# The last feed-forward product taken by k tiles first, and the first operands of the second half made inside the last quad

## The chip, the cores and the metric

The kernel runs on one core of one Trainium2 chip. The metric is the device time of one launch, in microseconds. Five engines run side by side, each through its own list of instructions in order: PE (matrix products; its weight loads are PEld), DVE and ACT (elementwise work), POOL (a slower elementwise engine) and SP, which here only issues DMAs.

## The reference, cut to what matters

One transformer block on x (1024 tokens of 1024 channels, fp32), a token mixer and then a gated feed-forward. The change touches only the feed-forward and the final norm:

```python
a, g = jnp.split(h @ w_ffn_in, 2, axis=-1)      # h: 1024 x 1024, w_ffn_in: 1024 x 5632
y    = (jax.nn.silu(g) * a) @ w_ffn_out          # w_ffn_out: 2816 x 1024
x    = x + g2 * y
out  = _rmsnorm(x, final_norm_g)                 # over the 1024 channels of a token
```

## The kernel before, in words

Products are fp32 made of three passes: each operand is split into a high part (a cast, on ACT, L637) and a low part (raw minus high, on DVE, L638), and PE multiplies high by high, high by low and low by high (`PASS`). Each pass of a 128x128 by 128x512 step is one matmul. Big products are done by a 2x2 block scheme with seven block products instead of eight, which needs sums and differences of blocks before and after.

The first half of the feed-forward runs 22 "quads" (`todo`, `run_quads`). A quad makes 128 rows of a and 128 rows of g for all 1024 tokens from seven products of 12 matmuls: A11 (`ahead_1`), S3, A12 (`ahead_2`, called by `others` as `mid`), S2, S1, A22 and S4. Its weights come as two raw tiles (`weights`, L689), are split (`weights_a`, L236/L237) and summed and split again (`weights_s`, L700 to L710). After S2, S1, A22 and S4 DVE adds the products up (L741, L744, L747, L750), POOL one of them (L742), ACT applies silu (L1257), DVE multiplies (L1261), and the result goes to DRAM as `actd`. Each of the four results of a quad is 128x512.

The second half is act @ w_ffn_out by 512x512 quarters with k split in 11 pairs of tiles. Seven block products run in the order P1, P7, P2, P6, P5, P4, P3 (`quarter`, L1285), each 11 k tiles x 4 token tiles x 3 passes = 132 matmuls into four PSUM banks, k outermost. `prepared(name)` loads the operands of k + 1 (L1213; an activation tile and a weight tile of 256 KB each), combines them where the scheme asks for it (L1227, L1231, L1235, L1240), and splits those of k. Raw tiles alternate between a pool of three buffers (named wr) and one of four (wr2), the same two pools that the quads' weights use; split tiles live in a pool of 40 (named s). While a product runs, the steps in its `side` list are interleaved: results of earlier products are taken out of PSUM and joined to the residual (L1300, L1301).

Two places matter here. `f_hook` runs after a quad. In quad 20 (counted from 0, the last but one) it makes the row of g2 (`row_of`: 16 small matmuls into two PSUM banks, L1006, and two copies, L1007) and the operands of P1 for k = 0, with the loads for k = 1. And the last product, P3, has a loop of its own: all 11 operands are prepared first, with the sums of P4's result (L1354) and `finish` of token tiles 4 to 7 between them; then token tile by token tile all k are multiplied (L1368), and each of the token tiles 0 to 3 is joined and finished: two sums of squares on ACT (L1307), a square root on POOL (L172), two scalings on DVE (L1311) and two stores (L1312).

The order of instructions on each engine is set by a scheduler that starts from the order of the program text: what stands earlier in the text takes buffers first.

Of the kernel before, what the change touches and what calls it, by code (L numbers as in the profile page):

```python
# [29 lines left out]
NF = DFF // P  # L30
# [3 lines left out]
def block_kernel(  # L34
# [63 lines left out]
    def gbank(shape=(P, 512)):  # L98
        return psg.tile(list(shape), F32, tag="g", name=nm("g"))
# [527 lines left out]
    def pe(ins):  # L627

        if last_pe[0] is not None:
            tc.add_manual_dep(ins.ins, last_pe[0].name, mybir.DependencyInfo(mybir.DependencyClass.NoSync, mybir.DependencyReason.DATA), reason="pe")  # L630
        last_pe[0] = ins.ins
        return ins

    def parts_of(raw, shape=(P, 2, 512)):

        hi, lo = slot(list(shape), F32R), slot(list(shape), F32R)
        nc.scalar.copy(hi, raw)  # L637
        nc.vector.tensor_sub(lo, raw, f(hi))  # L638
        return hi, lo
# [45 lines left out]
    def weights(w, cols):  # L685
        got = []
        for c0 in cols:
            t = raw_w([P, KT, P])
            nc.sync.dma_start(t, w[:, c0:c0 + P].rearrange("(k p) f -> p k f", p=P))  # L689
            got.append(t)  # L690
        return got

    def weights_a(va):
        hi, lo = split_w(va, [P, KT, P])
        return {"A11": (hi[:, 0:4, :], lo[:, 0:4, :]), "A12": (hi[:, 4:8, :], lo[:, 4:8, :])}

    def weights_s(va, ga, ops, eng):
        a11, a12, a21, a22 = va[:, 0:4, :], va[:, 4:8, :], ga[:, 0:4, :], ga[:, 4:8, :]
        s32, s14 = slot([P, 2, 4, P]), slot([P, 2, 4, P])
        nc.vector.tensor_sub(s32[:, 0], a11, a21)  # L700
        nc.vector.tensor_sub(s32[:, 1], a22, s32[:, 0])
        eng.tensor_add(s14[:, 0], s32[:, 1], a11)
        eng.tensor_sub(s14[:, 1], a12, s32[:, 1])
        for t, names in ((s32, ("S3", "S2")), (s14, ("S1", "S4"))):
            hi, lo = parts_of(t, (P, 2, 4, P))
            for i, name in enumerate(names):
                ops[name] = hi[:, i], lo[:, i]
        both = slot([P, 2, 4, P], F32R)
        nc.scalar.copy(both[:, 0], a22)
        nc.vector.tensor_sub(both[:, 1], a22, f(both[:, 0]))  # L710
        ops["A22"] = both[:, 0], both[:, 1]

    def product(ps, wts, mov, start):
        for k in range(4):
            for i, (a, b) in enumerate(PASS):
                pe(nc.tensor.matmul(ps, wts[a][:, k, :], mov[k // 2][b][:, k % 2, :], start=start and k == 0 and i == 0, stop=k == 3 and i == 2, skip_group_check=True))  # L716

    def tmp(s):
        return small.tile([P, 512], F32, tag="ev", name=nm(s), bufs=ev_bufs)

    def ahead_1(q, op, get_bank):
        q["A"] = get_bank()
        product(q["A"], q["ops"]["A11"], op["B11"], True)
        if q.get("p1") is None:
            q["p1"] = tmp("p1")
        nc.scalar.copy(q["p1"], q["A"])

    def ahead_2(q, op):
        product(q["A"], q["ops"]["A12"], op["B21"], False)

    def others(q, op, sink, mid=None):

        ops, p1 = q["ops"], q["p1"]
        X, Y, q7, u3 = banks[1](), banks[1](), tmp("q7"), tmp("u3")
        product(X, ops["S3"], op["T3"], True)
        nc.scalar.copy(q7, X)  # L736
        if mid:
            mid()
        sink(1, 1, q["A"])
        product(X, ops["S2"], op["T2"], False)  # L740
        nc.vector.tensor_add(u3, X, p1)  # L741
        nc.gpsimd.tensor_sub(q7, u3, q7)  # L742
        product(Y, ops["S1"], op["T1"], True)
        nc.vector.tensor_add(u3, Y, u3)  # L744
        sink(2, 2, u3)
        product(X, ops["A22"], op["T4"], False)
        nc.vector.tensor_add(p1, X, p1)  # L747
        sink(2, 1, p1)
        product(Y, ops["S4"], op["B22"], False)
        nc.vector.tensor_add(q7, Y, q7)  # L750
        sink(1, 2, q7)
# [12 lines left out]
    def run_quads(op, todo, quads, hook=None):  # L764

        for fi, (w, cols, sink) in enumerate(todo):
            if fi < len(quads):
                if fi:
                    weights_s(*weights(w, cols), quads[fi]["ops"], nc.vector)
                others(quads[fi], op, sink)  # L770
            else:
                va, ga = weights(w, cols)
                q = {"ops": weights_a(va)}
                weights_s(va, ga, q["ops"], nc.gpsimd)
                ahead_1(q, op, banks[0])
                others(q, op, sink, lambda: ahead_2(q, op))
            if hook:
                hook(fi)

    def half(t):  # L780
        return slice((t - 1) * 512, t * 512)
# [217 lines left out]
    def row_of(col):  # L999

        row = slot([P, D])
        for hf in range(2):
            pb = gbank((P, 4, P))
            for j in range(4):
                k = 4 * hf + j
                nc.tensor.matmul(pb[:, j, :], col[:, k:k + 1].to_broadcast([P, P]), ident, start=j == 0, stop=True, skip_group_check=True)  # L1006
            nc.vector.tensor_copy(row[:, hf * 512:(hf + 1) * 512], pb.rearrange("p j i -> p (j i)"))  # L1007
        return row

    next_small("small_h")  # L1010
    run_quads(h_op, todo, quads)


    KH = NF // 2
# [201 lines left out]
    def operands(name, k):  # L1216

        k2 = k + KH
        s = sk[k // 2][:, k % 2, :]
        if name == "P1":  # L1220
            return raw_tile(act_q(k, 0), w_q(k, 0))
        if name == "P2":
            return raw_tile(act_q(k2, 0), w_q(k2, 0))
        if name == "P7":
            t, r = raw_tile(act_q(k, 0), wsum[k]["T3"]), tmp("a21")
            nc.sync.dma_start(r, act_q(k, 1))
            nc.vector.tensor_sub(t[:, 0, :], t[:, 0, :], r)  # L1227
            nc.scalar.copy(s, t[:, 0, :])
        elif name == "P6":
            t = raw_tile(act_q(k2, 1), wsum[k]["T2"])  # L1230
            nc.vector.tensor_sub(t[:, 0, :], t[:, 0, :], s)  # L1231
            nc.scalar.copy(s, t[:, 0, :])
        elif name == "P5":
            t = raw_tile(act_q(k, 0), wsum[k]["T1"])
            nc.vector.tensor_add(t[:, 0, :], t[:, 0, :], s)  # L1235
        elif name == "P4":
            t = raw_tile(act_q(k2, 1), wsum[k]["T4"])
        else:
            t = raw_tile(act_q(k2, 0), w_q(k2, 1))
            nc.vector.tensor_sub(t[:, 0, :], t[:, 0, :], s)  # L1240
        return t

    def prepared(name):

        t = operands(name, 0)
        for k in range(KH):
            t, now = operands(name, k + 1) if k + 1 < KH else None, t
            yield parts_of(now)
# [15 lines left out]

    def f_hook(fi):
        nonlocal g2r
        if fi == NF - 2:
            g2r = row_of(g2)
            early.append(next(gen))

# [8 lines left out]
    def quarter(gen, banks, start, side=(), per=2):  # L1279

        side = list(side)
        for k, o in enumerate(gen):
            for tt in range(4):
                for i, (a, b) in enumerate(PASS):
                    pe(nc.tensor.matmul(banks[tt], o[b][:, 0, tt * P:(tt + 1) * P], o[a][:, 1, :], start=start and k == 0 and i == 0, stop=k == KH - 1 and i == 2, skip_group_check=True))  # L1285
            if k >= 1:
                for _ in range(per):
                    if side:
                        side.pop(0)()
        for s in side:  # L1290
            s()
# [6 lines left out]
    def join(xt, sl, src):  # L1298
        t = tmp("gj")
        nc.vector.tensor_mul(t, src, g2r[:, sl])  # L1300
        nc.vector.tensor_add(xt[:, sl], xt[:, sl], t)  # L1301
# [14 lines left out]
    def later(fn, *tiles):  # L1316
        return [lambda tt=tt: fn(tt) for tt in range(4)]

    A, X = [gbank() for _ in range(4)], [bank() for _ in range(4)]
# [28 lines left out]
        nc.vector.tensor_add(u3[tt], Y[tt], u3[tt])  # L1348
        join(fin[4 + tt], rh, u3[tt])

    quarter(prepared("P4"), X, False, later(c22), 1)

    def c21(tt):
        nc.vector.tensor_add(p1[tt], X[tt], p1[tt])  # L1354
# [1 line left out]
        finish(4 + tt)  # L1356


    side = later(c21)
    o = []  # L1360
    for k, parts in enumerate(prepared("P3")):
        o.append(parts)
        if k >= 2 and side:
            side.pop(0)()
    for tt in range(4):
        for k in range(KH):
            for i, (a, b) in enumerate(PASS):
                pe(nc.tensor.matmul(Y[tt], o[k][b][:, 0, tt * P:(tt + 1) * P], o[k][a][:, 1, :], start=False, stop=k == KH - 1 and i == 2, skip_group_check=True))  # L1368
        join(fin[tt], rh, Y[tt])
        finish(tt)  # L1370

# [31 lines left out]
```

## Time and profile before

| what | us |
|---|---|
| device time, median of 3 runs (lowest, highest) | 1780.68 (1780.16, 1782.38) |
| device time of the profiled execution | 1779.25 |
| its span, first to last instruction | 1777.5 |
| PE busy in the span | 1712.9 (96%) |
| DVE, ACT, POOL busy | 1137.3, 668.5, 214.4 |

The profiled execution has 1.75 us around its span and lies 1.43 us below the median. In the profile a line such as L638 is a line of the kernel, a tile's name stands without its number, and "out<-in" says what is written from what. PE's matmuls overlap: the start of one to the start of the next is the time that one takes, and the length printed is longer by the end of its pipeline. A bracket at the end of a row says how long the engine was idle before it, and whose end released it.

### The profile page before, as it was taken

To read this page: it belongs to the slowest core of one execution; us is meant where nothing else is said; L and a number is where in the kernel's file an instruction comes from. 1 tells how busy PE (TensorE), PEld (TensorE's weight loads), DVE (VectorE), ACT (ScalarE), POOL (GpSimd) and SP (SyncE) were. 2 spreads that over 40 slices of the span, in tenths; PEclk is the share of its full clock that TensorE was granted. 3 is DMA by queue.
4 is the path that set the end of the run, shared out by engine and by line. 5 is a ranking of instruction groups with operands and counts; after the bars stand their busy time and mean duration, and the time that the engine had idled before them with its cause. 6 is when DMAs were issued, how large, how long until landed. Compare 5 with 4: busy or idle time off the path is not lost. (4 is left out here: it accounts for less than half of the span.)

```text
span 1777.5 us, 21603 instructions
## 1 busy us (share of the span) xinstructions
PE 1712.9 (96%) x8162; PEld 1407.4 (79%) x8162; DVE 1137.3 (64%) x1559; ACT 668.5 (38%) x974; POOL 214.4 (12%) x193
## 2 busy tenths in 40 slices
PE   8899999999899999999999999899999999899996
PEld 3887888887678888887888888678888888688885
DVE  7686595866964554377756745985555553646795
ACT  6663423423443433234322213533333332445352
POOL 2220000000112352000000000022212211100001
PEclk9999999999999999999999999999999999999998
DMA  9511234052354453487868942243222222568472
GB/s 342 153 36 36 95 108 178 24 178 60 113 165 125 137 171 119 143 307 243 269 209 298 325 159 83 69 124 92 83 75 92 83 76 79 178 226 287 144 249 95
DMA packets 219961, 267.89 MB, mean 151 GB/s; under 512 B 11920, under 2 KB 142032, under 8 KB 219856
## 3 DMA queue, kind: packets, MB, share of 16 engines
q1 hardware_dynamic: 219040, 265.08, 45.0%
q8 instruction: 64, 1.05, 0.2%
q0 software_dynamic: 720, 1.40, 0.2%
q14 instruction: 41, 0.34, 0.1%
q10 hardware_dynamic: 96, 0.02, 0.0%
HBM read 205.64 MB, written 60.82 MB: 150 GB/s over the span
## 5 line engine op out<-in xcount | busy, mean ns | idle before, releaser
L716 PE MATMUL m<-s,s 128*128 128x512 f32 x1320 | 310.8, 392 | 13.7 <-DVE s L638 4.1
L716 PEld LDWEIGHTS m<-s,s 128*128 128x128 f32 x1320 | 247.9, 189 | 70.8 <-DVE s L638 5.8
L273 PE MATMUL m<-s,whi 128*128 128x512 f32 (+1 forms) x832 | 253.2, 385 | 1.4 <-ACT s L992 0.7
L237 DVE TENSOR_TENSOR wlo<-wr,whi 128x1024 fp32r<-128x1024 f32 x92 | 112.4, 1224 | 195.1 <-ACT whi L236 188.4
L716 PE MATMUL g<-s,s 128*128 128x512 f32 x960 | 225.8, 393 | 8.0 <-ACT q L736 4.1
L716 PEld LDWEIGHTS g<-s,s 128*128 128x128 f32 x960 | 180.0, 189 | 50.5 <-ACT q L736 6.9
L273 PEld LDWEIGHTS m<-s,whi 128*128 128x128 f32 x832 | 154.9, 190 | 32.4 <-ACT s L992 1.6
L236 ACT CAST whi<-wr 128x1024 fp32r<-128x1024 f32 x92 | 96.4, 1051 | 211.7 <-PE m L273 105.4
L273 PE MATMUL m<-s,wlo 128*128 128x512 f32 (+1 forms) x416 | 159.5, 385 | 1.8 <-DVE rstd L171 1.8
L638 DVE TENSOR_TENSOR s<-s,s 128x1024 fp32r<-128x1024 f32 x98 | 144.6, 1486 | 12.6 <-ACT s L637 8.7
L637 ACT CAST s<-s 128x1024 fp32r<-128x1024 f32 x98 | 102.4, 1052 | 128.2 <-DVE s L638 59.8
L172 POOL TENSOR_TENSOR rstd<-rstd,nhalf 128x1 f32<-128x1 f32 (+2 forms) x43 | 29.2, 678 | 852.8 <-DVE rstd L171 852.7
L285 PE MATMUL m<-whi,s 128*128 128x256 f32 x640 | 126.4, 292 | 0.1
L716 PE MATMUL g<-s,whi 128*128 128x512 f32 x384 | 118.6, 390 | 0.0
L638 DVE TENSOR_TENSOR s<-wr,s 128x1024 fp32r<-128x1024 f32 x77 | 91.2, 1220 | 30.4 <-ACT s L637 30.2
L285 PEld LDWEIGHTS m<-whi,s 128*128 128x128 f32 x640 | 101.9, 193 | 4.2 <-issue 2.7
L637 ACT CAST s<-wr 128x1024 fp32r<-128x1024 f32 x77 | 78.7, 1053 | 51.8 <-DVE wr L1235 19.0
L742 POOL TENSOR_TENSOR q<-u,q 128x512 f32<-128x512 f32 x38 | 59.4, 1562 | 314.4 <-DVE u L741 164.0
L285 PE MATMUL m<-wlo,s 128*128 128x256 f32 x320 | 92.4, 289 | 1.4 <-DVE wlo L237 1.4
L273 PEld LDWEIGHTS m<-s,wlo 128*128 128x128 f32 x416 | 78.8, 189 | 16.6 <-DVE rstd L171 2.0
L1168 PE MATMUL m<-s,s 128*128 128x512 f32 x384 | 87.6, 390 | 0.0
L1168 PEld LDWEIGHTS m<-s,s 128*128 128x128 f32 x384 | 72.0, 188 | 14.9
(293 smaller groups left out, 2879.8 us busy)
## 6 DMA issues: line engine op xcount, KB each, us to landing
wr<-in_w_in_dram SPq DMA_DIRECT2D x82, 512.0 KB
s<-in_w_ada_dram SPq DMA_DIRECT2D x48, 512.0 KB
wr<-in_w_ffn_in_dram SPq DMA_DIRECT2D x48, 512.0 KB
wr<-actd SPq DMA_DIRECT2D x77, 256.0 KB
s<-in_w_ffn_out_dram SPq DMA_DIRECT2D x22, 512.0 KB
wsT<-s SPq DMA_DIRECT2D x44, 256.0 KB
wr<-wsT SPq DMA_DIRECT2D x44, 256.0 KB
wr<-in_w_ffn_out_dram SPq DMA_DIRECT2D x33, 256.0 KB
```

What stands on the lines that cost most here:

```text
L172: nc.gpsimd.tensor_tensor(r[:, :n], r[:, :n], nhalf[:, :n], op=ALU.pow)
L236: nc.scalar.copy(hi, raw)
L237: lo_sub[0] = nc.vector.tensor_sub(lo, raw, f(hi)).ins
L273: nc.tensor.matmul(ps, ws[a][:, k, :], get(b, k, t0, n), start=k == 0 and i == 0, stop=k == nk - 1 and i == 2)
L285: nc.tensor.matmul(ps[:, j, :], get(b, 4 * kh + k, (2 * tp + j) * P, P), ws[a][:, k, :], start=kh == 0 and j == 0 and k == 0 and i == 0, s ...
L637: nc.scalar.copy(hi, raw)
L638: nc.vector.tensor_sub(lo, raw, f(hi))
L716: pe(nc.tensor.matmul(ps, wts[a][:, k, :], mov[k // 2][b][:, k % 2, :], start=start and k == 0 and i == 0, stop=k == 3 and i == 2, skip_gr ...
L742: nc.gpsimd.tensor_sub(q7, u3, q7)
L1168: pe(nc.tensor.matmul(ps, yF.get(b, k, tt * P, P), wo[k // 2][a][:, k % 2, :], start=k == 0 and i == 0, stop=k == KT - 1 and i == 2))
```

## The change

`f_hook` now acts at the last quad, 21, and it is called from inside it: `others` calls `ahead_2` and then the hook, so g2's row and P1's first operands stand behind the last quad's weights in the text, after A12. Of P3, the operands of k = 0, 1 and 2 are made in three side steps of P4. Its first five k tiles are multiplied k by k, each for all four token tiles, with the other operands and the `side` steps between; the last six k tiles are multiplied token tile by token tile as before, each followed by its join and finish.

```diff
@@ run_quads
-                others(q, op, sink, lambda: ahead_2(q, op))
-            if hook:
-                hook(fi)
+                others(q, op, sink, lambda: (ahead_2(q, op), hook and hook(fi)))
@@ f_hook
-        if fi == NF - 2:
+        if fi == NF - 1:
             g2r = row_of(g2)
             early.append(next(gen))
@@ second half
-    quarter(prepared("P4"), X, False, later(c22), 1)
+    gen3, o = prepared("P3"), []
+    quarter(prepared("P4"), X, False, later(c22) + [lambda: o.append(next(gen3))] * 3, 1)
...
-    side = later(c21)
-    o = []
-    for k, parts in enumerate(prepared("P3")):
-        o.append(parts)
-        if k >= 2 and side:
-            side.pop(0)()
-    for tt in range(4):
-        for k in range(KH):
+    side, step = later(c21), 5
+
+    def last_product(tt, ks):
+        for k in ks:
             for i, (a, b) in enumerate(PASS):
                 pe(nc.tensor.matmul(Y[tt], o[k][b][:, 0, tt * P:(tt + 1) * P], o[k][a][:, 1, :], start=False, stop=k == KH - 1 and i == 2, skip_group_check=True))
+
+    for k in range(step):
+        while len(o) < k + 3:
+            o.append(next(gen3))
+        for tt in range(4):
+            last_product(tt, (k,))
+        if k >= 1:
+            side.pop(0)()
+    o.extend(gen3)
+    for tt in range(4):
+        last_product(tt, range(step, KH))
         join(fin[tt], rh, Y[tt])
         finish(tt)
```

No engine gets an instruction more or less (7522 rows on PE before and after, 1512 on DVE). What moves is shown at three places. Line numbers of the changed kernel are two lower up to L1339 (L1300 is L1298 there), L1354 is L1353, and L1368 is L1363.

First DVE, in the last quads, before: from P1's first low part (`s_1931`) to the last quad's first sum (L741). `wr_1932` and `wr_1933` are the last quad's weights, the five L638 rows above L741 low parts of P1's k = 1 to 5.

```order
L638 TENSOR_TENSOR s_1931_11819<-wr_1928_11812,s_1930_11818 128x1024
L700 TENSOR_TENSOR s_1936_11830<-wr_1932_11822,wr_1933_11824 128x512
L701 TENSOR_TENSOR s_1936_11830<-wr_1933_11824,s_1936_11830 128x512
L638 TENSOR_TENSOR s_1939_11837<-s_1936_11830,s_1938_11836 128x1024
L638 TENSOR_TENSOR s_1941_11841<-s_1937_11831,s_1940_11840 128x1024
L710 TENSOR_TENSOR s_1942_11844<-wr_1933_11824,s_1942_11844 128x512
L638 TENSOR_TENSOR s_1959_11974<-wr2_1929_11815,s_1958_11973 128x1024
L638 TENSOR_TENSOR s_1962_11993<-wr_1957_11970,s_1961_11992 128x1024
L638 TENSOR_TENSOR s_1965_12012<-wr2_1960_11989,s_1964_12011 128x1024
L638 TENSOR_TENSOR s_1968_12031<-wr_1963_12008,s_1967_12030 128x1024
L638 TENSOR_TENSOR s_1971_12050<-wr2_1966_12027,s_1970_12049 128x1024
L741 TENSOR_TENSOR u3_1948_11865<-m_1945_11862,p1_1944_11860 128x512
```

The same stretch of DVE now, from the copies of g2's row on.

```order
L1005 COPY s_1942_11868<-g_1943_11869 128x512
L1005 COPY s_1942_11868<-g_1944_11875 128x512
L638 TENSOR_TENSOR s_1948_11888<-wr_1945_11881,s_1947_11887 128x1024
L638 TENSOR_TENSOR s_1959_11974<-wr2_1946_11884,s_1958_11973 128x1024
L741 TENSOR_TENSOR u3_1941_11842<-m_1938_11839,p1_1937_11837 128x512
L638 TENSOR_TENSOR s_1962_11993<-wr_1957_11970,s_1961_11992 128x1024
L638 TENSOR_TENSOR s_1965_12012<-wr2_1960_11989,s_1964_12011 128x1024
L744 TENSOR_TENSOR u3_1941_11842<-m_1939_11840,u3_1941_11842 128x512
L638 TENSOR_TENSOR s_1968_12031<-wr_1963_12008,s_1967_12030 128x1024
L638 TENSOR_TENSOR s_1971_12050<-wr2_1966_12027,s_1970_12049 128x1024
L747 TENSOR_TENSOR p1_1937_11837<-m_1938_11839,p1_1937_11837 128x512
L638 TENSOR_TENSOR s_1974_12069<-wr_1969_12046,s_1973_12068 128x1024
```

The last quad's weight sums (L700 to L710) now stand one quad earlier, and between two of its result sums stand two low parts of P1, where five stood ahead of the first. Then come two more, L1261 for p1, L750, one, and the last L1261.

Second SP's issues behind the residual loads of P4's time, before: P4's operands of k = 7 to 10 (wsT is P4's prepared weight block), then P3's.

```order
L1213 DMA wr_2180_13272<-actd18_8985 128x512
L1213 DMA wr_2180_13272<-wsT47_6187 128x512
L1213 DMA wr2_2183_13291<-actd19_8986 128x512
L1213 DMA wr2_2183_13291<-wsT48_6191 128x512
L1213 DMA wr_2186_13310<-actd20_8987 128x512
L1213 DMA wr_2186_13310<-wsT49_6195 128x512
L1213 DMA wr2_2189_13329<-actd21_8988 128x512
L1213 DMA wr2_2189_13329<-wsT410_6199 128x512
L1213 DMA wr2_2195_13368<-actd12_8979 128x512
L1213 DMA wr2_2195_13368<-in_w_ffn_out_dram 128x512
L1213 DMA wr_2194_13364<-actd11_8978 128x512
L1213 DMA wr_2194_13364<-in_w_ffn_out_dram 128x512
```

And now:

```order
L1211 DMA wr_2180_13272<-actd11_8978 128x512
L1211 DMA wr_2180_13272<-in_w_ffn_out_dram 128x512
L1211 DMA wr2_2181_13276<-actd12_8979 128x512
L1211 DMA wr2_2181_13276<-in_w_ffn_out_dram 128x512
L1211 DMA wr_2184_13284<-actd18_8985 128x512
L1211 DMA wr_2184_13284<-wsT47_6187 128x512
L1211 DMA wr2_2187_13303<-actd13_8980 128x512
L1211 DMA wr2_2187_13303<-in_w_ffn_out_dram 128x512
L1211 DMA wr2_2193_13330<-actd14_8981 128x512
L1211 DMA wr2_2193_13330<-in_w_ffn_out_dram 128x512
L1211 DMA wr_2190_13311<-actd19_8986 128x512
L1211 DMA wr_2190_13311<-wsT48_6191 128x512
```

P3's first four operands (actd11 to actd14) now stand ahead of P4's k = 8, 9 and 10; the last two of these follow the rows shown.

Third PE in the last product, before: bank `g_2112` (token tile 0) through its k tiles.

```order
L1368 MATMUL g_2112_12887<-s_2196_13372 128x512
L1368 MATMUL g_2112_12887<-s_2196_13372,s_2197_13373 128x512
L1368 MATMUL g_2112_12887<-s_2197_13373,s_2196_13372 128x512
L1368 MATMUL g_2112_12887<-s_2199_13380 128x512
L1368 MATMUL g_2112_12887<-s_2199_13380,s_2200_13381 128x512
L1368 MATMUL g_2112_12887<-s_2200_13381,s_2199_13380 128x512
```

And now: k = 0 through the banks `g_2112` to `g_2115`, of which the first two are shown, and then the place where k = 4 ends and the token-tile order begins.

```order
L1363 MATMUL g_2112_12887<-s_2182_13280 128x512
L1363 MATMUL g_2112_12887<-s_2182_13280,s_2183_13281 128x512
L1363 MATMUL g_2112_12887<-s_2183_13281,s_2182_13280 128x512
L1363 MATMUL g_2113_12888<-s_2182_13280 128x512
L1363 MATMUL g_2113_12888<-s_2182_13280,s_2183_13281 128x512
...
L1363 MATMUL g_2115_12890<-s_2212_13444,s_2211_13443 128x512
L1363 MATMUL g_2112_12887<-s_2217_13478 128x512
L1363 MATMUL g_2112_12887<-s_2217_13478,s_2218_13479 128x512
L1363 MATMUL g_2112_12887<-s_2218_13479,s_2217_13478 128x512
L1363 MATMUL g_2112_12887<-s_2223_13513 128x512
```

60 matmuls come k by k, 72 token tile by token tile. On DVE the last 28 rows ahead of token tile 0's join, from the sums of P4's result (L1354) on, stand as before.

## Rows read from the trace of the kernel before

**Rows 1.** Chain of waits: start, length (us), what; the transfers that it runs through.
```profile
1536.80 5.54 DMA wr<-in_w_ffn_out_dram
...
1580.62 29.92 PE m L1285 x132
...
1692.94 7.92 DMA s<-x2d
...
1711.76 3.70 DMA wr<-in_w_ffn_out_dram
```
**Rows 2.** Timeline of PE, quads 20 and 21: start, length, line, operation, count [idle before].
```profile
1503.34 0.61 PE L716 MATMUL g<-s,whi 128*128 128x512 f32 x2
...
1522.38 1.95 PE L1006 MATMUL g<-ident,mod 128*128 128x128 f32 x16
1524.08 0.71 PE L716 MATMUL g<-s,whi 128*128 128x512 f32 x2
...
1528.78 0.73 PE L716 MATMUL m<-s,s 128*128 128x512 f32 x2 [1.70 <-ACT s L637]
...
1543.70 6.04 PE L716 MATMUL m<-s,s 128*128 128x512 f32 x24 [2.55 <-DVE u L741]
1549.57 0.39 PE L1285 MATMUL g<-s 128*128 128x512 f32 x1
...
1552.45 0.50 PE L1285 MATMUL g<-s 128*128 128x512 f32 x1 [0.68 <-DVE p L1261]
```
**Rows 3.** Timeline of DVE in the same stretch.
```profile
1514.47 0.69 DVE L741 TENSOR_TENSOR u<-m,p 128x512 f32<-128x512 f32 x1 [1.77 <-PE m L716]
...
1523.91 1.28 DVE L1007 COPY s<-g 128x512 f32<-128x512 f32 x2
...
1541.82 1.23 DVE L638 TENSOR_TENSOR s<-wr,s 128x1024 fp32r<-128x1024 f32 x1 [2.96 <-ACT s L637]
```
**Rows 4.** Timeline of ACT in the same stretch.
```profile
1540.74 4.04 ACT L637 CAST s<-wr 128x1024 fp32r<-128x1024 f32 x4 [3.48 <-DMA wr<-in_w_ffn_out_dram]
```
**Rows 5.** Timeline of SP, issues only.
```profile
1467.15 0.34 SPq L1213 DMA_DIRECT2D wr<-actd  x1
...
1485.01 0.38 SPq L689 DMA_DIRECT2D wr<-in_w_ffn_in_dram  x1
...
1511.69 0.32 SPq L1213 DMA_DIRECT2D wr<-actd  x1
```
**Rows 6.** Timeline of PE, the last product P3 (L1368).
```profile
1730.06 0.39 PE L1368 MATMUL g<-s 128*128 128x512 f32 x1
...
1743.91 1.22 PE L1368 MATMUL g<-s,s 128*128 128x512 f32 x2 [7.34 <-DVE s L638]
1744.93 0.63 PE L1368 MATMUL g<-s 128*128 128x512 f32 x1
1745.36 1.06 PE L1368 MATMUL g<-s,s 128*128 128x512 f32 x2
```
**Rows 7.** Timeline of DVE from P5's results to the end.
```profile
1705.60 6.90 DVE L638 TENSOR_TENSOR s<-wr,s 128x1024 fp32r<-128x1024 f32 x6
...
1728.79 1.28 DVE L1354 TENSOR_TENSOR s<-m,s 128x512 f32<-128x512 f32 x2
...
1743.84 1.22 DVE L638 TENSOR_TENSOR s<-wr,s 128x1024 fp32r<-128x1024 f32 x1
...
1746.83 0.68 DVE L1300 TENSOR_TENSOR gj<-g,s 128x512 f32<-128x512 f32 x1
...
1769.36 0.69 DVE L1300 TENSOR_TENSOR gj<-g,s 128x512 f32<-128x512 f32 x1 [2.72 <-PE g L1368]
...
1772.70 1.41 DVE L1311 SCALAR_TENSOR_TENSOR s<-s,rstd,s 128x512 f32<-128x512 f32 x2 [0.73 <-POOL rstd L172]
```
**Rows 8.** Busy time by stretch: stretch, length, busy (count) of PE, PEld, DVE, ACT, POOL, PEclk, DMA share, GB/s.
```profile
1580.00:1610.00 30.00, 30.00 (x134) 24.86 (x133) 14.05 (x13) 16.30 (x24) 0.60 (x1) 1.00 0.63 211
1720.00:1744.00 24.00, 16.66 (x75) 13.47 (x73) 22.66 (x40) 12.26 (x23) 2.79 (x3) 0.92 0.35 127
```

## The prediction, made before the changed kernel ran

> **What bounds the kernel now.** I read the chain of waits first: its long pieces are whole products on PE, each starting where the last ends, 132 matmuls in 29.92 us [rows 1]. So one matmul costs 0.2267 us, 12 cost 2.72, a quad of 84 costs 19.04, and whatever makes PE wait is paid in full, except at the very end. The timeline of PE then shows where it waits in the part that the change touches: in the last quad [rows 2] and in the last product P3 [rows 6]. Between the two the stretch 1580 to 1610 stands for the rest: PE is busy in all of it at granted clock 1.00, that is the level of 2.4 GHz [rows 8].
>
> The last quad should take 19.04 us from 1524.08, and it takes until 1549.57, 25.49 us: 6.45 lost, of which 1.70 (before S3, for a weight part) and 2.55 (before A22, for DVE's L741) are printed as waits [rows 2]. P1 then waits 0.68, in its first k tile, for the PSUM bank that the last quad's L1261 reads, and P7 starts at 1580.62 instead of 1549.57 + 29.92 = 1579.49, so another 1.13 is lost [rows 1, 2]. The cause stands in the other timelines: P1's first operand was loaded at 1467.15, ahead of the last quad's weights, the second tile of which was issued only at 1485.01 [rows 5]; and DVE's low parts of P1's k = 1 to 5 stand ahead of L741, one of them held 2.96 us by a cast which ACT could not start for 3.48 us because a load was missing [rows 3, 4].
>
> In P3, PE multiplies token tile 0 up to k = 8 and then stands still 7.34 us until DVE has made the low part of k = 9, 1743.91; it restarts at half pace (0.43 us from 1744.93 to 1745.36, the level of 1.2 GHz; the stretch has 0.92 as its mean clock) [rows 6, 8]. Without that P3 would be issued until 1730.06 + 29.92 = 1759.98, and DVE could take its last result some 0.20 later, 1760.18; it takes it at 1769.36 [rows 7].
>
> **The last quad, step by step.** Its weights are now loaded and split a quad earlier, like those of every quad before, and these ran without a gap (1503.34 to 1522.38 is 19.04) [rows 2]. PE therefore starts A11 at 1522.38, S3 at 1525.10, A12 at 1527.82, then g2's row, which is moved and not removed: 1.70 us (1522.38 to 1524.08 before) [rows 2]. S2 starts at 1532.24, S1 at 1534.96, A22 at 1537.68, S4 at 1540.40, P1 at 1543.12, which is 6.45 earlier.
>
> DVE must keep up. A 128x512 op costs it 0.60 (two in 1.28, the last one's end included), a 128x1024 low part 1.14 (six in 6.90) [rows 7]; a result sum follows the product's end by 0.25 (L741 at 1514.47 for S2 issued until 1514.22) [rows 3]. The new order gives: copies of g2's row 1531.7 to 1533.1; low parts of k = 0 and 1 to 1535.4; L741 to 1536.1 (A22 needs it at 1537.68); k = 2 and 3 to 1538.3; L744 to 1539.0 (S4 needs it at 1540.40); k = 4 and 5 to 1541.2; L747 to 1541.9; k = 6 and 7 to 1544.1, which covers ACT's silu; L1261 to 1544.8. P1's fourth bank is the one that this frees, and PE comes to it at 1543.12 + 2.04 = 1545.16. So no wait is left, by margins of 1.6, 1.4 and 0.4 us. The queue moved past is SP's: k = 0 to 4 are issued by 1513, into buffers that free as the one at 1511.69 did [rows 5]; k = 5 and 7 wait for A12's end, 1530.54, k = 6 for the low part of k = 0, about 1534.4. With 3.70 us to land [rows 1] each is there before ACT is free for it. Then P1 is saved 6.45 + 1.13 = 7.58 us, and all of P7 to P4 moves up by it, since PE is never idle there. The bounds: nothing better than 7.58, as that is all that PE lost there; and if loads take the 7.92 us of the slowest row [rows 1], k = 6 lands at 1543.1, its cast and that of k = 7 (1.0 each [rows 4]) stand ahead of the silu, L1261 ends at 1547.1, PE waits 2.0, and 5.6 remain. I take 7.5: the loads of that time are two or three in flight, fewer than in the burst that took 5.54 [rows 1], and even with 5.54 the sums above stay.
>
> **P3, step by step, in times of the kernel before (all 7.5 earlier).** PE runs k = 0 to 4 for four token tiles, 60 matmuls, 13.60 us, 1730.06 to 1743.66. Token tile 0 ends 18 matmuls later, 1747.74; it needs the low part of k = 9 at 1746.38 and of k = 10 at 1747.06, which DVE has ready by 1743.84 and 1745.06 [rows 7]. DVE's list from P5's results to there has the same ops in another order, so it ends when it did if P4's and P3's loads come in time. P4's k = 8, 9 and 10 are now issued 12 us later, when DVE frees a buffer: about 1706.9, 1709.9 and 1711.0. With 3.70 to land, a cast of 1.0 and a low part, they are done by 1718.4, and PE needs them at 1721.90 to 1727.34. So the 7.34 of waiting and the slow restart go, and PE's last result is there at 1760.18 instead of 1769.36: 9.2.
>
> What is late next is the finish. From a token tile's join (L1300) to the second scaling DVE is in one chain through ACT and POOL: 1769.36 to 1774.11, and the next join may start after 4.68 (0.67 into the second of the pair at 1772.70) [rows 7]. Before, PE brought a token tile every 33 matmuls, 7.48; now every 18, 4.08, and DVE cannot follow. Token tile 0 joins at 1747.94 (PE's end plus 0.20, later than the 1746.83 when DVE is free [rows 7]); token tile 3 at 1747.94 + 3 x 4.68 = 1761.98 instead of 1769.36: 7.4 saved, and the last stores follow as before. Of the 9.2 on PE 1.8 is lost again behind DVE.
>
> **Sum.** 7.5 + 7.4 = 14.9. The profiled execution took 1779.25 (span 1777.5), so 1764.35; the median shown, 1780.68, lies 1.43 above it, so 1765.8 for a median.
>
> The Trainium skill, page "TensorE: Matmul & The Clock Gate", section "Loop structure matters more than you think", would keep the loop that P3 had: output tile outside, k inside, so that matmuls run back to back, and warns of loops in which every k tile waits. Here the trace differs: the products P1 to P4 have k outside and run at 0.2267 and clock 1.00 [rows 1, 8], and it is P3 with k inside that waits and restarts at half pace [rows 6]. What counts here is which operand is late, not the nesting.
>
> **Rivals.**
> (a) Loads bound. If they take 7.92 us instead of 3.70, the start keeps 5.6; and in P4's time k = 9's low part ends at 1720.4 instead of 1717.3, later ones follow, DVE's list is 3.8 late, of which 1.1 is slack: 2.7 of the tail go. 14.9 - 1.9 - 2.7 = 10.3, 1770.4. For it: DMA share 0.63 with PE fully busy [rows 8]. Against it: 7.92 is for 512 KB tiles behind each other.
> (b) Only one half works, for a buffer or a bank that I put wrongly: 7.4 or 7.5 alone, 1773.
> (c) Slower. The three wr buffers make a ring: low part of P4's k = 5, load of P4's k = 8, its low part, load of P3's k = 6, its low part, load of P3's k = 10. Each turn costs a landing plus some 3.1 (issue 0.8, cast 1.0, low part 1.2). Three turns from 1706.8 reach 1745.06, where k = 10 is due, only with landings of 9.6, and eat all 14.9 from about 15 us on; with 16 k = 10 comes at 1764.1, 19.0 late, less 1.1 slack: 1780.68 - 14.9 + 17.9 = 1783.7. No row lands that late.
> (d) The half clock in P3: k outside makes PE stop at each k tile and 60 matmuls cost 0.43. Then 12.2 more, 1778.0, no change. Against it [rows 8]. This is what the section of the Trainium skill named above warns of.
> (e) The finish runs at PE's pace, 4.08 per token tile: 1.8 better, 1764.0. Against it, DVE's list has no other work between the steps of one token tile.
>
> **Chances.** Forecast 0.66, (a) 0.12, (b) 0.07, (c) 0.03, (d) 0.02, (e) 0.10. Within 0.2% (3.6 us), which is about what this kernel's measurement can tell from no change, lies only (d). The range, 1762 to 1771, takes in (e), (a) and the bounds of both terms; (b), (c) and (d) stay outside. Faster 0.95, same 0.02, slower 0.03.
>
> **What would show it.** In the changed trace: P1 starts about 19.04 + 1.70 after the last quad's A11, with no wait of PE over 0.5 us between; P7 starts about 7.5 earlier; the row of g2 lies between A12 and S2; P3 runs 132 matmuls in 29.9 us with no idle time and clock 1.00; the joins of token tiles 0 to 3 follow each other by 4.7 us and each waits for DVE's own chain and not for PE; from PE's last matmul to the end it takes about 10 us instead of 8.2. I am wrong if P1 waits for a bank or a load, if P4 has gaps before k = 8 to 10, or if the joins wait for PE.

## The result, and the profile after

The changed kernel took 1767.87 us (median of 4 runs, 1766.73 to 1771.97) beside 1780.42 for the kernel before (1779.12 to 1782.38): ratio 0.993, 95% interval 0.9912 to 0.9948, 12.5 us less. Timed again in the experiment below it took 1766.92 beside 1782.39, ratio 0.9913 (0.9900 to 0.9926), 15.5 us less. The forecast was 1765.8, 14.9 less, with a range of 1762 to 1771.

The profiled execution of the changed kernel is the longest of its four, 1771.97 with a span of 1770.2. Both traces hold 8162 PE and 1559 DVE instructions (the text on the change has 7522 and 1512), so nothing was added or removed. I compare first the places that the change touches and then what lies ahead of them.

**The last quad and P1.** Timeline of PE, from the last quad's A11 to P1 (columns as in [rows 2]):

```profile
1529.25 0.61 PE L716 MATMUL g<-s,whi 128*128 128x512 f32 x2
...
1537.41 1.95 PE L1004 MATMUL g<-ident,mod 128*128 128x128 f32 x16
1539.11 11.16 PE L716 MATMUL m<-s,s 128*128 128x512 f32 x48
1550.11 0.39 PE L1283 MATMUL g<-s 128*128 128x512 f32 x1
...
1552.71 0.50 PE L1283 MATMUL g<-s 128*128 128x512 f32 x1 [0.40 <-DVE p L1259]
```

The row of g2 lies between A12 and S2, 36 matmuls (8.16 us) after the start of A11 at 1529.25. S2, S1, A22 and S4 are one group of 48 without a wait. The waits of 1.70 and 2.55 us of [rows 2] are gone. One wait is left, that of P1 for its fourth bank. The chain of waits gives the products behind it:

```profile
1552.71 28.20 PE g L1283 x123
1580.90 29.92 PE m L1283 x132
...
1700.58 29.92 PE m L1283 x132
1730.50 17.69 PE g L1363 x78
```

P7 starts 1580.90 - 1529.25 = 51.65 us after the last quad began; before it was 1580.62 - 1522.38 = 58.24 [rows 1, 2]. So 6.59 us came from here; 7.5 were forecast.

**The tail.** Windows of the changed kernel (columns as in [rows 8]):

```profile
1580.00:1610.00 30.00, 30.00 (x134) 24.83 (x134) 14.06 (x13) 16.30 (x23) 0.60 (x1) 1.00 0.64 211
1720.00:1744.00 24.00, 24.00 (x108) 19.88 (x107) 22.65 (x39) 12.35 (x23) 2.79 (x3) 1.00 0.40 144
```

The first stretch stands for the products between the two places and is as before. PE is busy in all of the second one, at granted clock 1.00; before it was 16.66 of 24 at 0.92 [rows 8]. The finish on DVE, from the last low part of P3 to the last scaling (timeline):

```profile
1744.04 1.22 DVE L638 TENSOR_TENSOR s<-wr,s 128x1024 fp32r<-128x1024 f32 x1
...
1748.22 0.69 DVE L1298 TENSOR_TENSOR gj<-g,s 128x512 f32<-128x512 f32 x1 [1.10 <-PE g L1363]
...
1752.83 0.69 DVE L1298 TENSOR_TENSOR gj<-g,s 128x512 f32<-128x512 f32 x1
...
1757.43 0.69 DVE L1298 TENSOR_TENSOR gj<-g,s 128x512 f32<-128x512 f32 x1
...
1762.11 0.68 DVE L1298 TENSOR_TENSOR gj<-g,s 128x512 f32<-128x512 f32 x1
...
1764.36 0.16 DVE L1306 TENSOR_TENSOR ss<-ss 128x1 f32<-128x1 f32 x1 [0.85 <-ACT s L1305]
1764.56 0.15 DVE L171 TENSOR_SCALAR rstd<-ss 128x1 f32<-128x1 f32 x1
1765.44 1.41 DVE L1309 SCALAR_TENSOR_TENSOR s<-s,rstd,s 128x512 f32<-128x512 f32 x2 [0.73 <-POOL rstd L172]
```

P3's first matmul in the timeline of PE:

```profile
1730.34 0.39 PE L1363 MATMUL g<-s 128*128 128x512 f32 x1
```

Only the first join (L1298) waits for PE; the others follow at 4.61, 4.60 and 4.68 us behind DVE's own steps. The last join comes 31.77 us after P3's first matmul, the end 39.86. Before it was 39.30 and 47.44 (1769.36 and 1777.5 less 1730.06) [rows 6, 7]. So 7.58 us came from the tail; 7.4 were forecast.

**What lies ahead.** From the beginning of the last quad (before: of g2's row ahead of it) to the end it takes 240.95 us instead of 255.12: 14.17 less. But in this execution the last quad began 6.87 us later than in the profiled one of before, in work that stands in the same order in both. The largest piece, 4.0 us, comes where the quads begin. Windows of before, then of after:

```profile
1160.00:1165.00 5.00, 5.00 (x24) 4.13 (x23) 4.97 (x7) 0.52 (x1) 1.60 (x1) 1.00 0.54 159
```
```profile
1160.00:1165.00 5.00, 4.28 (x10) 2.88 (x10) 3.55 (x5) 2.43 (x4) 0.00 (x0) 0.50 0.50 143
```

After some waits (2.65 us the longest, at 1157.85) PE ran here at granted clock 0.50, the level of 1.2 GHz, where before it was back at 1.00. A group of matmuls behind it starts at 1179.75 instead of 1172.74: the delay is 7.0 us there and 6.9 at the last quad.

### The profile page after: what moved, and what is told of

Its sections match the earlier page's. It is cut to its first block, busy times and chain, and to the rows that moved or that the text cites. A ratio compares the mean times of both kernels' runs of the same rounds, so it can differ in the third digit from the quotient of the medians.

```text
span 1770.2 us, 21603 instructions
## 1 busy us (share of the span) xinstructions
PE 1712.4 (97%) x8162; PEld 1407.5 (80%) x8162; DVE 1138.8 (64%) x1559; ACT 668.5 (38%) x974; POOL 215.4 (12%) x193
## 4 chain that ended last, share of the span: by engine, by line
PE 79%; DVE 11%; DMA 4%; issue 3%; ACT 3%; POOL 1%; SPq 0%; DVEq 0%; ACTq 0%; POOLq 0%
PE m L716 20%; PE g L716 17%; PE m L273 13%; PE m L1283 5%; PE g L1283 5%; PE m L1166 5%; PE m L285 4%; PE g L538 2%; DVE s L638 1%; PE m L822 1%; DVE wlo L237 1%; DVE s L422 1%; PE g L822 1%; DMA s<-in_w_ada_dram 1%; PE g L1363 1%
## 5 line engine op out<-in xcount | busy, mean ns | idle before, releaser
L638 DVE TENSOR_TENSOR s<-s,s 128x1024 fp32r<-128x1024 f32 x98 | 145.4, 1494 | 9.9 <-ACT s L637 6.0
L638 DVE TENSOR_TENSOR s<-wr,s 128x1024 fp32r<-128x1024 f32 x77 | 92.3, 1233 | 22.8 <-ACT s L637 22.1
L742 POOL TENSOR_TENSOR q<-u,q 128x512 f32<-128x512 f32 x38 | 59.4, 1563 | 314.1 <-DVE u L741 150.3
L1166 PEld LDWEIGHTS m<-s,s 128*128 128x128 f32 x384 | 72.0, 188 | 14.9
```

The costliest lines, as they stand in the source:

```text
L1166: pe(nc.tensor.matmul(ps, yF.get(b, k, tt * P, P), wo[k // 2][a][:, k % 2, :], start=k == 0 and i == 0, stop=k == KT - 1 and i == 2))
```

## The experiments

The table has four times of each profile: from the last quad's first matmul (or g2's row, where that stands ahead) to P7's start; from P3's first matmul to the last join and to the end; and from the last quad's beginning to the end, which leaves out the part ahead. Ratios are to the kernel before, timed beside each.

| kernel | quad to P7 | P3 to last join | P3 to end | quad to end | median | ratio (95%) |
|---|---|---|---|---|---|---|
| before | 58.24 | 39.30 | 47.44 | 255.12 | 1780.42 to 1782.55 | 1 |
| after | 51.65 | 31.77 | 39.86 | 240.95 | 1767.87 | 0.993 (0.9912, 0.9948) |
| e0 after again | 51.67 | 31.77 | 39.94 | 241.05 | 1766.92 | 0.9913 (0.9900, 0.9926) |
| e1 quad only | 51.67 | 40.57 | 48.69 | 249.80 | 1776.25 | 0.9965 (0.9952, 0.9977) |
| e2 tail only | 57.70 | 31.76 | 39.90 | 247.04 | 1774.11 | 0.9957 (0.9943, 0.9970) |
| e3 L742 on DVE | 50.94 | 31.76 | 39.90 | 240.28 | 1767.34 | 0.9918 (0.9906, 0.9930) |
| e4 border 7 | 51.63 | 31.72 | 40.84 | 241.91 | 1770.02 | 0.9926 (0.9911, 0.9940) |
| e5 border 4 | 51.66 | 30.57 | 38.74 | 239.84 | 1767.49 | 0.9914 (0.9899, 0.9929) |
| e6 none early | 51.64 | 31.76 | 39.87 | 240.94 | 1768.48 | 0.9919 (0.9904, 0.9934) |
| e7 border 0 | 51.67 | 39.11 | 47.29 | 248.40 | 1775.19 | 0.9957 (0.9940, 0.9973) |
| e8 e3 + e5 | 50.95 | 30.69 | 38.88 | 239.26 | 1766.57 | 0.9915 (0.9901, 0.9929) |
| e9 held scaling | 51.64 | 30.12 | 38.22 | 239.29 | 1765.48 | 0.9918 (0.9904, 0.9932) |
| e10 e5 + e9 + e3 | 50.94 | 30.15 | 38.35 | 238.73 | 1766.78 | 0.9917 (0.9905, 0.9930) |

**e0, the changed kernel again.** No edit.

> The changed kernel once more, nothing edited. In its first profile the two changed places gave back 6.6 us (last quad and P1) and 7.6 us (tail), 14.2 together, but 6.9 us were lost ahead of them, by 1205 us, in instructions that stand in the same order in both kernels. Theory: that loss differs from execution to execution, mostly by how long PE runs at 1.2 GHz between 1150 and 1170 us; a new profile shows less of it, and the time comes near 1780.4 - 14.2 = 1766 us. Rival: the change itself delays the early part (other addresses, other buffers); then the loss of about 7 us ahead of 1205 us stands again in this profile.

The last quad began at 1524.55, 4.7 us earlier than in the first profile and 2.2 later than in that of before, while both changed places repeat within 0.1 us. In the twelve profiles of changed kernels it began between 1524.06 and 1529.25. So most of the 6.9 us differs from execution to execution. The one profile of before (1522.38) lies below all twelve, but that execution, 1779.25, is itself 1.2 to 3.3 us shorter than the medians of before; whether a small rest of the delay comes with the change isn't settled. The medians show none: 12.5 and 15.5 lie on both sides of 14.2, with intervals of 2 to 3 us either way.

**e1 and e2, each half alone.** e1 moves only the hook, e2 undoes only that:

```diff
-                others(q, op, sink, lambda: ahead_2(q, op))
-            if hook:
-                hook(fi)
+                others(q, op, sink, lambda: (ahead_2(q, op), hook and hook(fi)))
-        if fi == NF - 2:
+        if fi == NF - 1:
```

> Only the moved hook (g2's row and P1's first operand inside the last quad); P4 and P3 as in the kernel before. Theory: the last quad takes 20.74 us from its A11 to P1 instead of 27.19 with the row ahead of it, P1 keeps a loss of about 1 us, so 6.6 us less than the kernel before: 1773.8 us; P3 still waits some 7 us for the low part of k = 9. The forecast on record had 7.5 for this part. Rival: the gain is given back in the tail, because P3's late operands are late by the loads and not by DVE's list; then the wait in P3 grows to about 14 us and the time stays at 1780.

> Only P3 by k tiles first, with its first three operands made during P4; the hook stays at the last quad but one. Theory: 7.6 us less than the kernel before, 1772.8 us (the forecast on record had 7.4): the last quad keeps its waits of 1.70 and 2.55 us, P3 runs 132 matmuls in 29.9 us, the joins follow at 4.6 to 4.7 us. Rival: each half alone gives almost all of the gain, because both remove the same lateness of the loads; then this kernel lies below 1769.

The halves add up: ratios 0.9965 and 0.9957 are 6.2 and 7.7 us of 1782.4, 13.9 together, with some 2 us either way on each. By the profiles e2 gains 7.54 in the tail. Its last quad, the same code as before, takes 57.70 to P7 and not 58.24, because the wait for L741 was 1.93 instead of 2.55: so 0.5 us of that column differs from execution to execution. e1 gains 6.57 up to P7 and loses 1.25 again in P3: the wait there did not grow to 14 us, it is the old one, but PE is slower after it, in the window 1743.4 to 1747.4 at 0.65 of its clock, where the kernel before had 0.97 in the like one (1747 to 1751). Timeline and window of e1, then the window of before:

```profile
1740.27 1.22 PE L1366 MATMUL g<-s,s 128*128 128x512 f32 x2 [7.35 <-DVE rstd L171]
```
```profile
1743.40:1747.40 4.00, 4.00 (x13) 3.21 (x12) 2.42 (x6) 1.45 (x4) 0.55 (x1) 0.65 0.35 131
```
```profile
1747.00:1751.00 4.00, 4.00 (x18) 3.26 (x17) 2.42 (x6) 1.45 (x4) 0.55 (x1) 0.97 0.35 131
```

The rival for e2, that each half alone gives nearly everything, is out: 1774.11 is far from 1769.

**e3, the subtraction of L742 on DVE in the last quad.**

```diff
-    def others(q, op, sink, mid=None):
+    def others(q, op, sink, mid=None, eng=nc.gpsimd):
-        nc.gpsimd.tensor_sub(q7, u3, q7)
+        eng.tensor_sub(q7, u3, q7)
-                others(q, op, sink, lambda: (ahead_2(q, op), hook and hook(fi)))
+                others(q, op, sink, lambda: (ahead_2(q, op), hook and hook(fi)), nc.vector if hook and fi == len(todo) - 1 else nc.gpsimd)
```

> The changed kernel, with the subtraction of L742 (128x512) in the last quad moved from POOL to DVE; the other quads keep it on POOL. In the profile of the changed kernel two low parts of 128x1024 took 3.45 us while this POOL operation ran (2.35 elsewhere), and PE then waited for P1's fourth bank; P1 lost about 1.0 us. Theory: the two engines don't run such operations at the same time, so DVE loses the 1.1 us to POOL. With the operation on DVE for 0.60 the pair takes 2.3 and DVE's list is 0.5 us shorter, P1's wait of 0.40 goes, P7 starts 0.6 to 1.0 us earlier after the last quad's A11 than in the changed kernel (51.65), and the time falls by as much, too little to tell in the total. Rival: the pair is slow for another reason (loads, or the casts on ACT); then it stays at 3.4, DVE's list is 0.6 longer, and the wait in P1 grows from 0.4 to about 1 us.

The pair is no longer slow, and P7 starts 0.71 us earlier, as the theory said; but the list of DVE changed in a second way, which is told below. Timeline of DVE, then of POOL, in the changed kernel (the POOL row of 1522.17 is that of the quad before):

```profile
1540.00 2.35 DVE L638 TENSOR_TENSOR s<-wr,s 128x1024 fp32r<-128x1024 f32 x2
1542.27 0.68 DVE L741 TENSOR_TENSOR u<-m,p 128x512 f32<-128x512 f32 x1
1542.87 3.45 DVE L638 TENSOR_TENSOR s<-wr,s 128x1024 fp32r<-128x1024 f32 x2
1546.24 0.68 DVE L744 TENSOR_TENSOR u<-m,u 128x512 f32<-128x512 f32 x1
1546.84 2.34 DVE L638 TENSOR_TENSOR s<-wr,s 128x1024 fp32r<-128x1024 f32 x2
...
1549.71 2.34 DVE L638 TENSOR_TENSOR s<-wr,s 128x1024 fp32r<-128x1024 f32 x2
1551.97 0.68 DVE L1259 TENSOR_TENSOR p<-g,p 128x512 f32<-128x512 f32 x1
```
```profile
1522.17 1.29 POOL L742 TENSOR_TENSOR q<-u,q 128x512 f32<-128x512 f32 x1 [17.81 <-DVE u L741]
...
1543.08 2.15 POOL L742 TENSOR_TENSOR q<-u,q 128x512 f32<-128x512 f32 x1 [19.62 <-issue]
```

and of DVE in e3:

```profile
1538.34 1.22 DVE L638 TENSOR_TENSOR s<-wr,s 128x1024 fp32r<-128x1024 f32 x1
1539.47 0.69 DVE L742 TENSOR_TENSOR q<-u,q 128x512 f32<-128x512 f32 x1
1540.07 1.22 DVE L638 TENSOR_TENSOR s<-wr,s 128x1024 fp32r<-128x1024 f32 x1
1541.21 0.69 DVE L744 TENSOR_TENSOR u<-m,u 128x512 f32<-128x512 f32 x1
1541.81 1.22 DVE L638 TENSOR_TENSOR s<-wr,s 128x1024 fp32r<-128x1024 f32 x1
...
1543.67 2.35 DVE L638 TENSOR_TENSOR s<-wr,s 128x1024 fp32r<-128x1024 f32 x2
1545.94 0.68 DVE L1259 TENSOR_TENSOR p<-g,p 128x512 f32<-128x512 f32 x1
```

Two low parts of 128x1024 took 3.45 us beside L742 and 2.35 without. The times read as strict turns: the first low part ends at about 1544.0 (1542.87 + 1.14), POOL's operation, which takes 1.29 when DVE is idle (1522.17), then ends at 1545.23 (1543.08 + 2.15), the second low part at 1546.32. In e3 DVE reaches L1259 21.22 us after the last quad's first matmul instead of 22.72 (1545.94 and 1551.97 less 1524.72 and 1529.25), P1 has no wait, and P7 starts 0.71 us earlier. The Trainium skill, page "SBUF — State Buffer", section "SBUF: two separate sides", says why: DVE and GpSimd (POOL) share a pair of ports as an exclusive lock, and a DVE operation with two SBUF inputs is blocked by a GpSimd operation that reads SBUF for the whole of that instruction. The trace agrees, with 1.10 us lost on DVE.

The second way: in e3 one low part stands between L744 and L747 where the changed kernel has two, so L1259 has one fewer ahead of it. Of the 1.50 us by which L1259 comes earlier, 0.50 is L742's (L744 starts 16.49 instead of 16.99 us after the last quad's first matmul), and most of the rest is that low part. How much of P1's gain is L742's can be estimated from the rows: P1 was due at its fourth bank 9 matmuls after its start, at 1552.15, and came to it at 1552.71, 0.56 late; 0.50 earlier, it would have been 0.06 late. So L742 alone would have removed nearly all of the wait; that was not run by itself.

**e4 and e5, the border between the two loops of P3.** `side, step = later(c21), 5` with 7 and with 4, and the rest of `side` is emitted, with one operand ahead of each, where fewer than four fit:

```diff
-        if k >= 1:
+        if k >= 1 and side:
             side.pop(0)()
+    while side:
+        o.extend(itertools.islice(gen3, 1))
+        side.pop(0)()
     o.extend(gen3)
```

> The changed kernel with P3's border at 7 instead of 5: k = 0 to 6 for all four token tiles, then k = 7 to 10 token tile by token tile. Theory (the finish chain of DVE, ACT and POOL, 4.64 us per token tile, sets the tail): token tile 0 is there 7 x 2.72 + 12 x 0.227 + 0.2 = 22.0 us after P3's start, the last join 3 x 4.64 later, 35.9 instead of 31.8: 4.1 us slower than the changed kernel, about 1771 us. Rival (the finish keeps up with PE): PE's last result is at 30.1 us either way, the last join comes there, and the time is the same or 1.6 us better.

> The changed kernel with the border at 4: seven k tiles, 21 matmuls, 4.76 us, are left for each token tile, about as long as the finish chain. Theory: the joins wait only for DVE, which in the changed kernel is free 16.7 us after P3's start; the last one comes at 16.7 + 3 x 4.64 = 30.6 instead of 31.8 us, so 1.2 us of gain, 1766.9 - 1.2 = 1765.7, seen in the profile and hardly in the total. Rival: k = 9 and 10 are now needed 2.7 us earlier, at 14.3 and 15.0 us, where their low parts are ready at 13.7 and 14.9; if these slip, PE waits in token tile 0, falls to 1.2 GHz as in the kernel before, and the time is 2 to 5 us worse.

e5 came out as expected (30.57 for 30.6). e4 did not: the first join comes at 21.96 us, as it should, but the last at 31.72 and not at 35.9. Timeline of DVE in e4:

```profile
1749.32 0.69 DVE L1298 TENSOR_TENSOR gj<-g,s 128x512 f32<-128x512 f32 x1 [5.19 <-PE g L1363]
...
1753.93 0.68 DVE L1298 TENSOR_TENSOR gj<-g,s 128x512 f32<-128x512 f32 x1
1754.65 0.69 DVE L1299 TENSOR_TENSOR s<-s,gj 128x512 f32<-128x512 f32 x1
1755.26 0.68 DVE L1298 TENSOR_TENSOR gj<-g,s 128x512 f32<-128x512 f32 x1
...
1759.08 0.68 DVE L1298 TENSOR_TENSOR gj<-g,s 128x512 f32<-128x512 f32 x1
```

Token tile 2 joins 1.33 us after token tile 1, in the time in which DVE would wait for ACT's square: in e4's list the steps of two token tiles stand between each other. Why the scheduler chose that order here the runs don't show. So 4.64 us per token tile is not a floor of the finish; it comes from the order of DVE's list in the changed kernel. The total is 2 to 3 us above the changed kernel's, 1.0 by the profile; the intervals overlap.

**e6 and e7, which half of the tail's edit counts.** e6 takes the three early operands out; e7 is border 0, so the nesting of before with them:

```diff
-    quarter(prepared("P4"), X, False, later(c22) + [lambda: o.append(next(gen3))] * 3, 1)
+    quarter(prepared("P4"), X, False, later(c22), 1)
```

> The changed kernel without the three operands of P3 that are made among P4's; they are made after all of P4's, as in the kernel before, while P3 keeps its new order. Theory (the order of P3's matmuls gives the tail's gain, since it needs k = 9 and 10 only 16 us after the start): DVE's list has the same operations in another order, so PE waits at most 1 us at P3's start, and the time is 1767 to 1768 us. Rival (the early operands give it): P3 waits at its start for loads, 4 us or more, and the time is 1771 us or above.

> The changed kernel with the border at 0: P3 token tile by token tile, as in the kernel before, but with its first three operands made during P4. Theory: token tile 0 needs k = 9 and 10 at 6.1 and 6.8 us after P3's start, and DVE has them at about 13.7 and 14.9; PE waits about 8 us there, runs on at 1.2 GHz for a while, and the last join comes at 39 us instead of 31.8: 7.5 us slower than the changed kernel, about 1774.4. Rival (by the rule for loops with k inside, in the Trainium skill, TensorE: Matmul & The Clock Gate, section on loop structure, with the operands early it is the better order): no wait, the last join at 30.1 us, 1.7 us faster than the changed kernel.

e6 loses nothing (39.87 for 39.86), e7 loses 7.4 of the tail's 7.6 us. Timeline of PE in e7:

```profile
1739.39 1.22 PE L1363 MATMUL g<-s,s 128*128 128x512 f32 x2 [7.27 <-DVE rstd L171]
1740.41 0.63 PE L1363 MATMUL g<-s 128*128 128x512 f32 x1
1740.83 1.05 PE L1363 MATMUL g<-s,s 128*128 128x512 f32 x2
```

That is the wait of [rows 6] again, and the half pace behind it (0.42 us from 1740.41 to the next row at 1740.83). The order of P3's matmuls gives the whole gain, by needing k = 9 and 10 some 10 us later (16.3 and 17.0 instead of 6.1 and 6.8 us after its start); that operands are made early gives nothing here. The Trainium skill, page "TensorE: Matmul & The Clock Gate", section "Loop structure matters more than you think", shows as good a loop with output tiles outside and k inside, in which matmuls follow back to back, and as bad one with a long wait before every matmul. In this case it is the loop with k inside that has the wait, 7.27 us in e7, and the one with k outside that has none: what decides is which operand is late.

**e9, e8 and e10, DVE's list in the tail, and versions that could be faster.** e9 puts the second scaling of a token tile behind the next one's join (shortened: the helper that does one scaling, and ties it to that join, is left out, and the comments are added here):

```diff
-        join(fin[tt], rh, Y[tt])
-        finish(tt)
+        joined = join(fin[tt], rh, Y[tt])
+        if held:
+            held.pop()(joined)                    # scale(rh) of the token tile before, behind this join
+        finish(tt, held if tt < 3 else None)      # scales lh, and holds scale(rh) back
```

e8 is e5 and e3 together; e10 is e9 with border 4 and e3's edit.

> The changed kernel (border at 5) with one DVE operation moved: the second scaling of token tile 0, 1 and 2 stands behind the join of the next token tile, in the time in which DVE waits for ACT's square (0.85 us), instead of ahead of it. Theory (the tail of the changed kernel is bound by the order of DVE's list, in which nothing stands between the steps of one token tile, and not by the work in it): the joins follow PE at 4.08 instead of 4.64 us, the last one comes 17.9 + 3 x 4.08 = 30.1 us after P3's start instead of 31.8, and the end comes 38.2 instead of 39.9 us after it: 1.6 us less. Rival (the chain through ACT and POOL itself sets the pace): joins at 4.6 us as before, no gain.

> Two edits that gave back 1.1 and 0.7 us each by the profiles, together: the border of P3 at 4, and the subtraction of L742 on DVE in the last quad. Theory: they touch different stretches, so they add up: P7 starts 50.9 us after the last quad's A11 (51.65 in the changed kernel), the end comes 38.7 us after P3's start (39.9), and the median lies 1.8 us below the changed kernel's 1766.9 to 1767.9, at 1765 to 1766. Rival: P1's earlier start meets later loads, and one of the two gains is lost; then 1766.5 or more.

> All three edits: border of P3 at 4, the second scaling behind the next join, the subtraction of L742 on DVE in the last quad. Theory: with the border at 4 PE brings a token tile every 4.76 us and DVE keeps up, so the last join waits for PE: 30.1 us after P3's start, the end 38.2 us after it, P7 50.9 us after the last quad's A11: 1.6 + 0.7 = 2.3 us below the changed kernel, about 1765 us. Rival: with the border at 4 DVE is free only 16.7 us after P3's start and stays behind PE; then the end comes at 38.7, as without the second edit.

Joins in e9 (timeline of DVE):

```profile
1743.36 0.69 DVE L1298 TENSOR_TENSOR gj<-g,s 128x512 f32<-128x512 f32 x1 [1.11 <-PE g L1371]
...
1747.44 0.69 DVE L1298 TENSOR_TENSOR gj<-g,s 128x512 f32<-128x512 f32 x1
...
1751.52 0.69 DVE L1298 TENSOR_TENSOR gj<-g,s 128x512 f32<-128x512 f32 x1
...
1755.60 0.69 DVE L1298 TENSOR_TENSOR gj<-g,s 128x512 f32<-128x512 f32 x1
```

They follow at 4.08 us, PE's pace, and the last one is 30.12 us after P3's start, as forecast; 1.65 us of the tail with no work removed. By the profiles the edits nearly add up: e8 has both gains (50.95 and 38.88, for 50.9 and 38.7), and e10 takes 238.73 from the last quad to the end, 2.2 less than the changed kernel. But no median shows it, and that of e8 lies where its rival put it (1766.5 or more): 1765.48, 1766.57 and 1766.78 have ratios inside the changed kernel's interval.

## Why the prediction was right, and where its terms were off

- **Sum.** 14.9 forecast, 14.17 by the profiles from the last quad on, 12.5 and 15.5 by the medians. The two terms missed in opposite directions, 6.59 for 7.5 and 7.58 for 7.4. Both halves are there and independent (e1, e2), so rivals (b) and (c) are out; (d) is out by clock 1.00 in P3. (a) is out: S2 to S4 and P4 to P3 run without a wait. One reading in the chances was wrong: (c) at 1783.7 also lies within 3.6 us of 1780.68, not only (d).
- **Last quad.** The schedule of PE held to 0.1 us: A11 to P1 20.86, forecast 20.74. L741 came as forecast. L744 came 1.0 us late and still 0.5 ahead of S4; its margin should have been 1.4.
- **P1: the term that was mis-sized.** "k = 2 and 3 to 1538.3" has two low parts in 2.3 us; they took 3.45 beside POOL's L742, an operation that the sum of DVE's work left out. So L1259 came 0.9 late, and the margin of 0.4 at P1's fourth bank was gone. P1 takes 30.63 us from its first matmul to P7's, 0.71 more than 132 matmuls without a wait; the forecast had none of this. Of the 0.99 us between 7.58 and 6.59, 0.71 is this, 0.12 is the quad, and 0.16 could not be had: the 1.13 of the forecast is a start in the chain of waits (1580.62) less one worked out in the timeline, and the timeline has P7 0.16 earlier. P7's first matmul, before and now:

```profile
1580.46 0.39 PE L1285 MATMUL m<-s 128*128 128x512 f32 x1
```
```profile
1580.74 0.39 PE L1283 MATMUL m<-s 128*128 128x512 f32 x1
```

  In e3 the 0.71 is gone. The trace of before had the sign: all 23 of its low parts (L638) that took over 1.6 us, 2.27 to 2.33 where 1.2 is usual, stand beside POOL's L742, 17 of them in the 22 quads of the feed-forward. One of them, DVE, then POOL, of before:

```profile
1477.19 2.33 DVE L638 TENSOR_TENSOR s<-s,s 128x1024 fp32r<-128x1024 f32 x1 [0.17 <-ACT s L637]
```
```profile
1477.16 1.28 POOL L742 TENSOR_TENSOR q<-u,q 128x512 f32<-128x512 f32 x1 [6.07 <-ACT s L637]
```

- **P3.** 132 matmuls without a wait at clock 1.00, low parts of k = 9 and 10 ready 13.7 and 14.9 us after the start, as worked out. Joins at 4.6 to 4.7 us behind DVE, the end 9.8 us after PE's last matmul (1760.42 to 1770.2; about 10 forecast). 7.58 instead of 7.4. That it came so close owes something to luck: what the old loop costs differs from execution to execution, and in e1, which has it, it was 1.25 us more.
- **Rival (e)** did not come, and its reason was right as it stands: nothing else is in DVE's list between the steps of one token tile. e4 and e9 show that this is the list's order alone: one moved scaling brings nearly all of (e)'s 1.8 us (1.65 measured), which the prediction did not see.

## What to carry to other kernels

Where a product's last operands come late and its results are finished one by one, run k outside until the operands are there and output tiles outside from then on; of the three borders tried with the finish as it was (4, 5 and 7), the one where what is left per tile (4.76 us) is about as long as the finish of a tile (4.64) had the earliest end by the profiles, by 1.1 us. Before adding up a list of DVE operations, look at what POOL does in the same microseconds, and add the two where both work on SBUF alone. Where a finish goes through several engines, let a step of another tile stand in the time in which DVE waits.

## What the runs showed that I had not expected

DVE and POOL took strict turns on operations that read two SBUF tensors: 1.10 us of DVE lost to one POOL subtraction of 128x512, and POOL held until DVE's running operation had ended (2.15 instead of 1.29). After the same stop in P3 in before, e1 and e7 (7.34, 7.35 and 7.27 us long) PE went on at granted clock 0.50 and was back at 1.00 at 1747.2, 1746.2 and 1742.4, that is 3.3, 6.0 and 3.0 us after it went on: equal waits did not cost the same.
